# Rounding all rows of x and the second weights ahead of the squares of x, and splitting half of the v weights into another buffer

## The chip, the cores and the metric

The kernel runs on one core of a Trainium2 chip. The time is the device time of one execution in microseconds; several executions are made and their median is compared. The engines are named as in the profile: PE is TensorE's matmul, PEld its weight load, DVE is VectorE, ACT is ScalarE, POOL is GpSimd, SP is SyncE, which issues almost all DMA transfers here.

## The reference

One inference step of a hybrid decoder layer on 512 prompt tokens and 64 sample tokens, 576 in all, with 1024 features. What matters here is the beginning: the input is normalized and then projected by one wide weight matrix, of which the first pieces used are those of a gated linear recurrence (HGRN).

```python
def rms_norm(x, g):
    xf = x.astype(jnp.float32)
    y = xf * lax.rsqrt(jnp.mean(xf * xf, axis=-1, keepdims=True) + EPS)
    return (y * g.astype(jnp.float32)).astype(x.dtype)
...
def mixer_features(h, pos, lb, w_in, q_norm_g, k_norm_g):
    B, T, _ = h.shape
    z = h @ w_in
    offs = np.cumsum(IN_WIDTHS)[:-1].tolist()
    q_a, kv_c, kv_s, kv_w, gate_a, q_b, f_b, i_b, g_b, mg = jnp.split(z, offs, axis=-1)
...
    logf = jnp.log(lb + (1.0 - lb) * jax.nn.sigmoid(fz)).reshape(B, T, B_HEADS, B_KEY_DIM)
...
    qb = jax.nn.silu(q_b.astype(jnp.float32)).reshape(B, T, B_HEADS, B_KEY_DIM)
    vb = i_b.astype(jnp.float32).reshape(B, T, B_HEADS, B_VAL_DIM)
    gb = jax.nn.silu(g_b)
```

After it come the recurrence for four heads, sparse attention for prompt and samples, a merge and a gated feed-forward part with a short convolution.

## The kernel before

Activations are kept transposed: features on the 128 partitions in eight tiles (`KT`), tokens along the free dimension. The products need nearly float32 precision and use a two-part form: a value is rounded by ACT to the matmul's 32-bit format (the high part) and DVE or POOL subtracts to get the remainder (the low part). `split` (lines 326 to 334) issues both steps. A product is then three matmuls, high by high, high by low and low by high, listed by `THREE`, and `gemm` (line 360) makes 48 matmuls of 288 columns for one weight tile of 1024 x 128 against all 576 tokens.

`prep_x` (line 478) loads the eight rows of x, scales and rounds them (ACT line 333, DVE line 334), squares each one (ACT line 500) and adds the squares into two accumulators, those of even rows on DVE and those of odd rows on POOL (line 505). The token sums (line 451) and `token_rms` (line 454: mean squares on DVE, a power on POOL, line 463) give one factor per token. These factors do not enter the rounded x: the projections use unnormalized x and are multiplied by the factors afterwards. `spread` (line 466) carries the factors from partitions to columns: DVE writes a diagonal matrix `dg` (line 472), PE multiplies it with ones (lines 474 and 475), and DVE copies the result to `rsb`.

`hgrn` (line 806) then runs head by head: `hgrn_inputs` projects f with the weights wF and q with wQ, `hgrn_values` projects v for two heads with wI (lines 528 and 532), and a projection with wG gives the output gate. Weights come through `wload` into a ring of two raw buffers (`wraw`), and `wsplit` (line 341) splits them into a ring of two split buffers (`wsp`); every third split gives its remainder to POOL instead of DVE. For the first head wQ and wG do not use the ring: they are split into `phi` and `plo`, the two buffers that later hold the split pages of the compressed cache. wF of the first head is loaded and split inside `prep_x`; `wcols` (line 352) loads and splits wI in two halves of four feature tiles each.

The order on each engine is not the order of the source: the tile framework's scheduler arranges the instructions by its own estimates, and each engine then runs its list strictly in that order. `issue_after(i)` makes what is issued inside it follow instruction i in the scheduler's order. The list of SP is one queue: a transfer that must wait for a buffer holds those behind it.

Of the kernel before, what the change touches and what calls it, by code (L numbers as in the profile page):

```python
# [13 lines left out]
AF = mybir.ActivationFunctionType  # L14
# [8 lines left out]
KT = 8  # L23
# [201 lines left out]
QPL = "phi"  # L225
# [62 lines left out]
class Layer:  # L288
# [60 lines left out]
        self.split(sp[:, 0], sp[:, 1], raw, eng=nc.gpsimd if self.nsplit % self.pool_every == 0 else nc.vector)  # L349
        return sp  # L350

    def wcols(self, dram, cols):

        out = []
        for k in range(0, KT, 4):
            sp = self.wsplit(dram[:, k:k + 4], 4, cols)
            out += [sp[:, :, i] for i in range(4)]
        return out

# [118 lines left out]
    def prep_x(self, p):  # L478

        nc, a = self.nc, self.a  # L480
        self.xg = [Rows([self.xp.tile([128, 4, T], F32R, name="xg", tag=f"hi{i}") for i in range(2)]),
                   self.xp.tile([128, KT, T], F32R, name="xg", tag="lo")]
        self.xs = self.w1p.tile([128, KT, 2, 64], F32R, name="xs")
        self.rsb = self.xp.tile([128, T], F32, name="rsb", tag="rsb")
        self.rst = self.xp.tile([128, 5], F32, name="rst")
        acc = []
        for k in range(KT):
            x = p.tile([128, T], F32, name="x", tag="x", bufs=8)
            with self.tc.issue_after(self.wdma.ins) if k == 2 else nullcontext():
                nc.sync.dma_start(x, a["xT"][:, k])  # L490
            if k == 0:
                self.load_consts(self.cp, "base")
            if k == 1:
                self.w_first = self.wsplit(a["wF"][0], KT, 128)
            self.split(self.xg[0][:, k], self.xg[1][:, k], x, scale=self.small[:, k:k + 1])
            sq = p.tile([128, T], F32, name="sq", tag="z", bufs=6)
            if k in SQP:
                nc.gpsimd.tensor_tensor(sq, x, x, op=ALU.mult)
            else:
                nc.scalar.activation(sq, x, AF.Square)  # L500
            c = k % 2
            if k < 2:
                acc.append(sq)
            else:
                (nc.gpsimd if k in ADP else nc.vector).tensor_tensor(acc[c], acc[c], sq, op=ALU.add)
        ps = self.bank("ps")
        for i in range(2):
            self.token_sums(ps, acc[i], i == 0)
        for c in range(2):
            if c:  # L510
                nc.scalar.copy(self.xs[:, :, c, :], self.xg[c][:, :, TP:T].bitcast(F32))
            else:
                for i in range(2):
                    nc.scalar.copy(self.xs[:, 4 * i:4 * i + 4, c, :], self.xg[c].tiles[i][:, :, TP:T].bitcast(F32))
        rt = self.token_rms(p, ps, D)
        nc.vector.tensor_copy(self.rst, rt)
        pa, pb = self.spread(p, rt)
        nc.vector.tensor_copy(self.rsb[:, 0:512], pa)
        nc.vector.tensor_copy(self.rsb[:, 512:576], pb[:, 0:64])
        self.tap("rsb", self.rsb)  # L520
# [60 lines left out]
    def hgrn_inputs(self, p, h, q):  # L581

        nc, a = self.nc, self.a
        f = p.tile([128, T], F32, name="f", tag="f", bufs=2)
        k = p.tile([128, T], F32, name="k", tag="k", bufs=2)
        mv = p.tile([128, 144, 10], F32, name="mv", tag="mv")
        z = self.project(self.wsplit(a["wF"][h], KT, 128) if h else self.w_first, p, 1.0)
        th = p.tile([128, T], F32, name="th", tag="th", bufs=2)
        nc.scalar.activation(th, z, AF.Tanh, scale=0.5)
        nc.gpsimd.tensor_scalar(f, th, self.fb[:, h:h + 1], self.fa[:, h:h + 1], op0=ALU.mult, op1=ALU.add)  # L590
        nc.gpsimd.tensor_scalar(k, th, self.fbn[:, h:h + 1], self.fb[:, h:h + 1], op0=ALU.mult, op1=ALU.add)
        z = self.project(self.wsplit(a["wQ"][h], KT, 128, QPL and not h and (q, QPL)), p, 0.5, "g" if h else "lv")
        self.silu2(mv[:, :, 0:4], z, p, j=4)
        return f, k, mv

    def hgrn_values(self, p, x):

        w = self.wcols(self.a["wI"][x], 256)
        for j in range(5):
            ps = self.bank("ps")  # L600
            self.gemm_tok(ps, w, 256, j)
            d = self.vb[0:128 if j < 4 else 64, j, x].rearrange("p a b -> p (a b)")
            self.tok_out([(d, 0, 256)], ps, 256, j, p, "s1")
# [202 lines left out]
    def hgrn(self, p, q):  # L806
        nc, a = self.nc, self.a
        self.lm = p.tile([128, 1184], U8, name="lm")
        lmf = p.tile([128, 1184], F32, name="lmf", tag="mv")
        with self.tc.issue_after(self.wdma.ins):  # L810
            nc.sync.dma_start(lmf, a["lmask"])
        nc.vector.tensor_copy(self.lm, lmf)
        self.hgrn_consts()
        self.vb = p.tile([128, 5, 2, 2, 128], F32, name="vb")
        nxt = self.hgrn_inputs(p, 0, q)
        self.cmp = None
        for h in range(4):
            self.h = h
            if h % 2 == 0:
                self.hgrn_values(p, h // 2)  # L820
            gz = self.project(self.wsplit(a["wG"][h], KT, 128, GPL and not h and (q, GPL)), p, 0.5)
            if h == 0:
                with self.tc.issue_after(self.wdma.ins):
                    self.cmp_weights(q)
            gb = p.tile([128, T], F32, name="gb", tag="gb")
            self.silu2(gb, gz, p)
            if h == 0:
                self.cmp = self.cmp_sample(q)
            self.step(0)
            po = self.hgrn_chain(p, h, *nxt)  # L830
            if h == 0:
                self.cmp_pos(q)
            self.step(2)
            self.readout(p, h, *po, gb)
            if h < 3:
                nxt = self.hgrn_inputs(p, h + 1, q)
            self.gates_a(p, range(GA[h], GA[h + 1]))
            self.step(3)
            if h < 2:
                with self.tc.issue_after(self.page_dma.ins):  # L840
                    for b in range(4 * h, 4 * h + 4):
                        nc.sync.dma_start(self.o["wins"][b, 0:504, :], a["wst"][b, 8:512, :])

        for _ in self.cmp:
            pass
# [1058 lines left out]
```

## Time and profile before

| what | value |
|---|---|
| median of 3 executions | 1139.88 us (1139.77 to 1142.56) |
| profiled execution, its own time | 1141.99 us |
| its span, first to last instruction | 1140.2 us |
| PE busy | 1092.3 us, 96% of the span |
| DVE, ACT, POOL busy | 658.1, 470.8, 430.4 us |
| mean granted clock of PE | 0.985 |

The span is the stretch from the first to the last instruction of one profiled execution; the execution's own time has 1.8 us more, which lie around it. Times in the rows below are counted from the span's start. An engine that is busy for a small share can still hold PE up where its work stands in a chain ahead of PE's.

### The profile page before, as it was taken

What the parts mean: (1) busy time and instruction counts of PE and PEld (TensorE: products, weight loads), DVE (VectorE), ACT (ScalarE), POOL (GpSimd) and SP (SyncE); (2) the same over time, 40 slices, a digit from 0 to 9 for tenths busy, and PEclk for the clock granted to TensorE, in tenths of its full rate; (3) what the DMA queues carried; (4) which work ended last, traced back from release to release, by engine and by line L of the source; (5) the groups of instructions that cost most, each with busy time, mean ns of one, the idle gap of its engine ahead of it and who ended that gap; (6) DMA issues with size and microseconds to landing.
All of it is one profiled execution on the core that took longest, in us unless ns stands there. A gap on an engine that the chain in (4) does not pass through costs nothing.

```text
span 1140.2 us, 21336 instructions
## 1 busy us (share of the span) xinstructions
PE 1092.3 (96%) x7936; PEld 1034.8 (91%) x7936; DVE 658.1 (58%) x1182; ACT 470.8 (41%) x929; POOL 430.4 (38%) x514
## 2 busy tenths in 40 slices
PE   5999999999999899999888799999999999999998
PEld 5997999898999899899665699999999999999998
DVE  6768555674257756887776664665555555511110
ACT  5523443443444567776565643332223222311110
POOL 3654513833374535343365354232223222301010
PEclk8999899999999999999899999999999999999999
DMA  5634456454342422273789675322232223334330
GB/s 199 185 103 155 126 160 194 131 156 149 124 148 59 131 88 72 77 224 101 222 274 284 208 220 183 93 91 88 79 93 75 85 83 93 99 104 124 102 115 21
DMA packets 99273, 151.54 MB, mean 133 GB/s; under 512 B 11233, under 2 KB 66274, under 8 KB 99042
## 3 DMA queue, kind: packets, MB, share of 16 engines
q1 hardware_dynamic: 97714, 146.00, 41.2%
q0 software_dynamic: 1024, 3.54, 1.0%
q8 instruction: 62, 1.02, 0.4%
q10 hardware_dynamic: 432, 0.65, 0.2%
q14 instruction: 41, 0.34, 0.1%
HBM read 131.65 MB, written 22.62 MB: 135 GB/s over the span
## 4 chain that ended last, share of the span: by engine, by line
PE 60%; DVE 6%; ACT 2%; DMA 1%; issue 1%; POOL 1%; SPq 0%; DVEq 0%; ACTq 0%; POOLq 0%
PE ps_g L367 44%; PE ps_g L1200 2%; PE ps_hp L1307 2%; PE ps_sb L1299 2%; PE ps_po L1634 1%; DVE r L1138 1%; PE ps_sa L1267 1%; PE ps_g L1763 1%; PE ps_g L1773 1%; POOL rr L1128 1%; PE ps_sm L1333 1%; PE ps_g L1333 1%; DMA nraw<-in_wk 1%; PE ps_sa L1260 0%; PE ps_sc L1551 0%
## 5 line engine op out<-in xcount | busy, mean ns | idle before, releaser
L367 PE MATMUL ps_g<-h,wsp 128*128 128x288 f32 x2112 | 279.8, 294 | 0.0
L367 PEld LDWEIGHTS ps_g<-h,wsp 128*128 128x128 f32 x2112 | 279.4, 188 | 0.1
L330 ACT CAST wsp<-wraw 128x1024 fp32r<-128x1024 f32 (+3 forms) x142 | 136.3, 966 | 281.0 <-PE ps_g L367 240.5
L367 PE MATMUL ps_g<-xg,wsp 128*128 128x288 f32 x1200 | 182.9, 305 | 16.4 <-ACT wsp L330 8.8
L367 PEld LDWEIGHTS ps_g<-xg,wsp 128*128 128x128 f32 x1200 | 167.7, 193 | 23.6 <-ACT wsp L330 9.0
L331 DVE TENSOR_TENSOR wsp<-wraw,wsp 128x1024 fp32r<-128x1024 f32 (+2 forms) x93 | 113.5, 1222 | 116.4 <-ACT wsp L330 116.1
L331 POOL TENSOR_TENSOR wsp<-wraw,wsp 128x1024 fp32r<-128x1024 f32 (+3 forms) x49 | 108.0, 2203 | 187.1 <-ACT wsp L330 183.7
L367 PE MATMUL ps_g<-g,wsp 128*128 128x288 f32 x1056 | 140.9, 296 | 0.0
L367 PEld LDWEIGHTS ps_g<-g,wsp 128*128 128x128 f32 x1056 | 140.8, 189 | 0.0
L528 PE MATMUL ps_t<-wsp,xg 128*128 128x262 f32 (+1 forms) x480 | 60.9, 285 | 0.0
L528 PEld LDWEIGHTS ps_t<-wsp,xg 128*128 128x128 f32 x480 | 58.9, 189 | 0.1
L903 PE MATMUL ps_pc<-phi,w 128*128 128x256 f32 x256 | 51.0, 290 | 0.0
L330 ACT CAST phi<-praw 128x2048 fp32r<-128x2048 f32 x16 | 30.4, 1901 | 45.7 <-PE ps_pc L903 27.6
L1848 POOL COPY cout<-ext 128x2 f32<-128x2 f32 x22 | 4.1, 184 | 119.0 <-DVE ext L1845 119.0
L1155 POOL TENSOR_TENSOR zg<-zg,rsb 128x576 f32<-128x576 f32 x16 | 27.2, 1699 | 56.4 <-ACT zg L1154 56.4
L1863 DVE TENSOR_TENSOR s<-ps_g,s 128x576 f32<-128x576 f32 x22 | 16.6, 757 | 51.5 <-POOL s L1859 51.5
L1855 ACT ACTIVATE s<-cv 128x512 f32<-128x512 f32 x22 | 13.9, 632 | 78.6 <-DVE cv L1853 78.6
L331 DVE TENSOR_TENSOR plo<-praw,phi 128x2048 fp32r<-128x2048 f32 x14 | 32.7, 2338 | 22.4 <-ACT phi L330 22.2
L903 PEld LDWEIGHTS ps_pc<-phi,w 128*128 128x128 f32 x256 | 42.1, 196 | 0.8 <-issue 0.8
L1274 ACT ACTIVATE sP<-sP,nm 128x128 f32<-128x128 f32 (+3 forms) x64 | 35.6, 560 | 9.2 <-DVE nm L1272 9.2
L1844 DVE TENSOR_TENSOR ext<-ps_g,rs 128x288 f32<-128x288 f32 x22 | 10.1, 457 | 50.8 <-PE ps_g L367 50.7
L1859 POOL TENSOR_TENSOR s<-s,rs 128x576 f32<-128x576 f32 x22 | 31.6, 1434 | 18.8 <-ACT s L1858 18.8
(428 smaller groups left out, 1983.0 us busy)
## 6 DMA issues: line engine op xcount, KB each, us to landing
wraw<-in_wFi SPq DMA_DIRECT2D x44, 512.0 KB
praw<-in_pc SPq DMA_DIRECT2D x256, 64.0 KB
praw<-in_pkv SPq DMA_DIRECT2D x80, 128.0 KB
wraw<-in_wM SPq DMA_DIRECT2D x16, 512.0 KB
wraw<-in_wFo SPq DMA_DIRECT2D x16, 512.0 KB
gbd<-zg SPq DMA_DIRECT2D x24, 288.0 KB
wraw<-in_wBr SPq DMA_DIRECT2D x24, 256.0 KB
pgs<-in_pkv SPq DMA_DIRECT2D x48, 128.0 KB
```

The costliest lines, as they stand in the source:

```text
L330: self.copied = nc.scalar.copy(hi, src)
L331: (eng or nc.vector).tensor_tensor(lo, src, hi.bitcast(F32), op=ALU.subtract)
L367: self.last = nc.tensor.matmul(ps[:, h, 0:HF], w[:, cw, wk, :], (x[cx] if isinstance(x, list) else x[:, cx])[:, xk, h * HF:(h + 1) * HF], ...
L528: nc.tensor.matmul(ps[:, 0:n], self.xg[cx][:, k, j * 128:j * 128 + 128], w[k][:, cw], start=(k == 0 and c == 0), stop=(k == KT - 1 and c = ...
L903: self.nc.tensor.matmul(ps, self.w1[:, cw, j, k], x[cx][:, k], start=start and k == 0 and n == 0, stop=k == 7 and n == 2, skip_group_check ...
L1155: nc.gpsimd.tensor_tensor(z, z, self.rsb, op=ALU.mult)
L1200: self.last = nc.tensor.matmul(ps, w[:, cw, k], self.obs[cx][:, k, c], start=n == 0, stop=n == 11)
L1274: nc.scalar.activation(s[:, b], s[:, b], AF.Exp, scale=-1.0, bias=nm[:, 1 + b, i:i + 1], accum_out=sm[:, 1 + b, i:i + 1])
L1299: nc.tensor.transpose(ps[:, n * 128:n * 128 + 128], sP[i][:, b, j * 128:j * 128 + 128], self.cst("ident"))
L1307: last = nc.tensor.matmul(po[:, i * 128:512], vs[:, j, b].rearrange("p a d -> p (a d)"), pt[:, c, n * 128:(n + m) * 128], start=first, sto ...
L1333: self.last = nc.tensor.matmul(ps, w[:, cw, k], self.oas0[:, cx, k], start=n == 0, stop=n == 11)
L1859: nc.gpsimd.tensor_tensor(s, s, self.rs2, op=ALU.mult)
```

## The change

The squares of x leave the loop that rounds x. A second loop makes them, after all rows are rounded and after the second weights, wQ of the first head, are loaded and split; the squares on ACT are ordered behind the cast of wQ (`self.copied`). wQ of the first head now uses the ring's buffer instead of `phi`, and the second half of the first wI is split into `phi` instead of into the ring.

```diff
-    def wcols(self, dram, cols):
+    def wcols(self, dram, cols, place=None):
 
         out = []
         for k in range(0, KT, 4):
-            sp = self.wsplit(dram[:, k:k + 4], 4, cols)
+            sp = self.wsplit(dram[:, k:k + 4], 4, cols, place if k else None)
...
-        acc = []
+        acc, xs = [], []
         for k in range(KT):
...
             self.split(self.xg[0][:, k], self.xg[1][:, k], x, scale=self.small[:, k:k + 1])
+            xs.append(x)
+
+        self.w_second = self.wsplit(a["wQ"][0], KT, 128)
+        for k, x in enumerate(xs):
             sq = p.tile([128, T], F32, name="sq", tag="z", bufs=6)
             if k in SQP:
                 nc.gpsimd.tensor_tensor(sq, x, x, op=ALU.mult)
             else:
-                nc.scalar.activation(sq, x, AF.Square)
+                with self.tc.issue_after(self.copied.ins):
+                    nc.scalar.activation(sq, x, AF.Square)
...
-        z = self.project(self.wsplit(a["wQ"][h], KT, 128, QPL and not h and (q, QPL)), p, 0.5, "g" if h else "lv")
+        z = self.project(self.wsplit(a["wQ"][h], KT, 128) if h else self.w_second, p, 0.5, "g" if h else "lv")
...
-    def hgrn_values(self, p, x):
-
-        w = self.wcols(self.a["wI"][x], 256)
+    def hgrn_values(self, p, x, q):
+
+        w = self.wcols(self.a["wI"][x], 256, None if x else (q, QPL))
...
-                self.hgrn_values(p, h // 2)
+                self.hgrn_values(p, h // 2, q)
```

The scheduler makes another order of this. Three places follow; lines behind 494 are numbered five higher in the changed kernel.

PE at the beginning, before the change. `ps_g` is the f projection, `ps_lv` the q projection, lines 451 the token sums, 474 and 475 the spread, 528 wI:

```order
L367 MATMUL ps_g<-xg,wsp 128x288 x44
L451 MATMUL ps_ps<-c_base,sq 128x2 x4
L451 MATMUL ps_ps<-c_base,sq 64x2
L367 MATMUL ps_g<-xg,wsp 128x288 x4
L367 MATMUL ps_lv<-xg,wsp 128x288 x4
L451 MATMUL ps_ps<-c_base,sq 128x2 x4
L451 MATMUL ps_ps<-c_base,sq 64x2
L367 MATMUL ps_lv<-xg,wsp 128x288 x44
L474 MATMUL ps_ps<-dg,c_base 128x512
L475 MATMUL ps_ps<-dg,c_base 128x64
L528 MATMUL ps_ps<-wsp,xg 128x256 x96
```

and with the change:

```order
L367 MATMUL ps_g<-xg,wsp 128x288 x48
L367 MATMUL ps_lv<-xg,wsp 128x288 x48
L451 MATMUL ps_ps<-c_base,sq 128x2 x4
L451 MATMUL ps_ps<-c_base,sq 64x2
L451 MATMUL ps_ps<-c_base,sq 128x2 x4
L451 MATMUL ps_ps<-c_base,sq 64x2
L474 MATMUL ps_ps<-dg,c_base 128x512
L475 MATMUL ps_ps<-dg,c_base 128x64
L533 MATMUL ps_ps<-wsp,xg 128x256 x96
```

The token sums stood inside f and q, with 44 matmuls of q between them and the spread; now they stand behind both, directly ahead of the spread.

DVE around the factors, before the change, from the remainder of wQ (`wraw_277`) on. `wraw_341` is the second half of wI, `wraw_471` is wG, `rst` and `dg` are the factors and their diagonal matrix, `ptab` the page table:

```order
L331 TENSOR_TENSOR wsp_279<-wraw_277,wsp_279 128x1024
L461 TENSOR_SCALAR ms_173<-ps_ps_159 128x4
L462 TENSOR_SCALAR ms_173<-ps_ps_159 64x1
L516 COPY rst_97<-rt_174 128x5
L472 TENSOR_SCALAR dg_180<-c_base_100,rt_174 128x128 x4
L472 TENSOR_SCALAR dg_180<-c_base_100,rt_174 64x64
L331 TENSOR_TENSOR wsp_343<-wraw_341,wsp_343 128x1024
L857 TENSOR_SCALAR ptab_527<-praw_t_528 1x128
L331 TENSOR_TENSOR wsp_473<-wraw_471,wsp_473 128x1024
L518 COPY rsb_96<-ps_ps_186 128x512
```

and with the change, again from the remainder of wQ (now `wraw_137`) on:

```order
L331 TENSOR_TENSOR wsp_139<-wraw_137,wsp_139 128x1024
L510 TENSOR_TENSOR sq_142<-sq_142,sq_146 128x576
L510 TENSOR_TENSOR sq_142<-sq_142,sq_152 128x576
L510 TENSOR_TENSOR sq_142<-sq_142,sq_158 128x576
L331 TENSOR_TENSOR wsp_343<-wraw_341,wsp_343 128x1024
L461 TENSOR_SCALAR ms_178<-ps_ps_164 128x4
L462 TENSOR_SCALAR ms_178<-ps_ps_164 64x1
L862 TENSOR_SCALAR ptab_527<-praw_t_528 1x128
L331 TENSOR_TENSOR wsp_473<-wraw_471,wsp_473 128x1024
L521 COPY rst_97<-rt_179 128x5
L472 TENSOR_SCALAR dg_185<-c_base_100,rt_179 128x128 x4
L472 TENSOR_SCALAR dg_185<-c_base_100,rt_179 64x64
```

The remainders of wI's second half and of wG stood behind `dg`; now they stand ahead of it, that of wI also ahead of the mean squares `ms`.

POOL's additions of squares, before the change (`wraw_336` is the first half of wI):

```order
L505 TENSOR_TENSOR sq_115<-sq_115,sq_128 128x576
L505 TENSOR_TENSOR sq_115<-sq_115,sq_142 128x576
L505 TENSOR_TENSOR sq_115<-sq_115,sq_156 128x576
L331 TENSOR_TENSOR wsp_338<-wraw_336,wsp_338 128x1024
L463 TENSOR_TENSOR rt_174<-ms_173,mhalf_62 128x5
```

and with the change:

```order
L510 TENSOR_TENSOR sq_144<-sq_144,sq_149 128x576
L510 TENSOR_TENSOR sq_144<-sq_144,sq_155 128x576
L331 TENSOR_TENSOR wsp_338<-wraw_336,wsp_338 128x1024
L510 TENSOR_TENSOR sq_144<-sq_144,sq_161 128x576
L463 TENSOR_TENSOR rt_179<-ms_178,mhalf_62 128x5
```

The remainder of wI's first half moved ahead of the last addition.

## Rows read from the trace of the kernel before

**Rows 1.** The page, busy time of an engine, share of the span and instructions.
```profile
PE 1092.3 (96%) x7936; PEld 1034.8 (91%) x7936; DVE 658.1 (58%) x1182; ACT 470.8 (41%) x929; POOL 430.4 (38%) x514
```

**Rows 2.** Timeline of PE: start us, us, engine line op, out<-in, count, [idle before <-releaser].
```profile
7.88 6.37 PE L367 MATMUL ps_g<-xg,wsp 128*128 128x288 f32 x32 [7.88 <-ACT wsp L330]
15.76 1.85 PE L367 MATMUL ps_g<-xg,wsp 128*128 128x288 f32 x12 [1.51 <-DVE xg L334]
...
24.81 7.80 PE L367 MATMUL ps_lv<-xg,wsp 128*128 128x288 f32 x44
32.45 1.02 PE L474 MATMUL ps_ps<-dg,c_base 128*128 128x512 f32 x2
...
33.76 11.50 PE L528 MATMUL ps_ps<-wsp,xg 128*128 128x256 f32 x96
...
47.00 6.54 PE L367 MATMUL ps_g<-xg,wsp 128*128 128x288 f32 x48
53.38 1.24 PE L672 MATMUL ps_lv<-mv,k 128*128 128x320 f32 x4
```

**Rows 3.** Timeline of DVE, 8 to 44 us.
```profile
10.41 0.81 DVE L334 SCALAR_TENSOR_TENSOR xg<-x,small,xg 128x576 fp32r<-128x576 f32 x1
...
16.36 1.99 DVE L505 TENSOR_TENSOR sq<-sq 128x576 f32<-128x576 f32 x1
18.27 2.89 DVE L334 SCALAR_TENSOR_TENSOR xg<-x,small,xg 128x576 fp32r<-128x576 f32 x1
21.08 1.21 DVE L331 TENSOR_TENSOR wsp<-wraw,wsp 128x1024 fp32r<-128x1024 f32 x1
...
26.53 0.17 DVE L516 COPY rst<-rt 128x5 f32<-128x5 f32 x1 [1.32 <-POOL rt L463]
26.61 1.02 DVE L472 TENSOR_SCALAR dg<-c_base,rt 128x128 f32<-128x128 f32 x5
...
42.27 0.47 DVE L659 TENSOR_TENSOR mv<-mv,f 128x144 f32<-128x144 f32 x1
```

**Rows 4.** Timeline of POOL, 8 to 27 us.
```profile
10.81 1.70 POOL L505 TENSOR_TENSOR sq<-sq 128x576 f32<-128x576 f32 x1 [9.72 <-ACT sq L500]
...
17.97 2.57 POOL L331 TENSOR_TENSOR wsp<-wraw,wsp 128x1024 fp32r<-128x1024 f32 x1 [0.24 <-ACT wsp L330]
25.29 1.21 POOL L463 TENSOR_TENSOR rt<-ms,mhalf 128x5 f32<-128x5 f32 x1 [4.75 <-DVE ms L462]
```

**Rows 5.** Timeline of ACT, 8 to 30 us.
```profile
8.14 0.78 ACT L333 ACTIVATE xg<-x,small 128x576 fp32r<-128x576 f32 x1 [0.32 <-DMA x<-in_xT]
...
12.86 0.67 ACT L500 ACTIVATE sq<-x 128x576 f32<-128x576 f32 x1
13.43 0.76 ACT L333 ACTIVATE xg<-x,small 128x576 fp32r<-128x576 f32 x1
...
27.05 1.04 ACT L330 CAST wsp<-wraw 128x1024 fp32r<-128x1024 f32 x1 [5.23 <-DMA wraw<-in_wI]
28.47 1.05 ACT L330 CAST wsp<-wraw 128x1024 fp32r<-128x1024 f32 x1 [0.38 <-DMA wraw<-in_wG]
```

**Rows 6.** Timeline of SP's queue: the requests of wI's second half and of wG.
```profile
22.32 0.33 SPq L338 DMA_DIRECT2D wraw<-in_wI  x1
22.75 0.37 SPq L338 DMA_DIRECT2D wraw<-in_wG  x1
```

**Rows 7.** Stretches: length, busy us (count) by engine, PE's granted clock, DMA share, GB/s.
```profile
12.00:13.00 1.00, 1.00 (x10) 1.00 (x9) 1.00 (x1) 1.00 (x3) 0.51 (x1) 1.00 0.97 397
13.00:14.00 1.00, 1.00 (x9) 0.97 (x8) 1.00 (x3) 1.00 (x2) 0.33 (x1) 1.00 0.16 61
...
21.80:28.60 6.80, 6.80 (x32) 6.77 (x31) 2.29 (x10) 1.19 (x3) 1.21 (x1) 0.50 0.73 230
...
110.70:114.00 3.30, 0.91 (x8) 0.56 (x6) 3.25 (x5) 1.25 (x4) 3.13 (x2) 0.99 0.86 293
114.00:117.40 3.40, 3.40 (x15) 3.40 (x16) 3.13 (x7) 1.92 (x6) 3.26 (x5) 0.51 0.73 246
```

## The prediction

> **What bounds the kernel now.** I read the page's busy times first: the matmul engine PE is busy for 96% of the span [rows 1], so a change pays only where it takes away a wait of PE or a stretch at PE's lower clock. Then PE's row of the timeline for the first 67 us, the only place that the change works on [rows 2]. Up to 24.8 us PE is in pieces (after 32 matmuls of f it waits 1.51 us for x rounded by DVE, and later again). From 24.81 us it runs without a wait: 44 matmuls of the q projection, the spread of the row factors, then from 33.76 us 96 matmuls on the v weights (wI). Third, why x is late: DVE rounds a row in 0.81 us, but the last one takes 2.89 us and ends at 21.16, because POOL runs a two-input operation beside it; a sum of squares on DVE takes 1.99 us for the same reason [rows 3], and POOL's operations are stretched likewise [rows 4]. Each waits for the other's whole operation. Fourth, the clock: after this broken stretch the granted clock is 0.50 from 21.8 to 28.6 us [rows 7], so 6.8 us of PE run at 1.2 instead of 2.4 GHz.
>
> **What the change moves.** The same instructions are issued; only order and two buffers change. On ACT the eight squares go behind the casts of x and of wQ; on DVE the eight roundings then follow each other; on POOL the remainder of wI's first half goes ahead of the last addition; PE runs f and q without the token sums between them. I follow one chain through this order, with durations from rows.
>
> *x and q, earlier.* The third row of x is cast at 8.14 us, on its landing [rows 5]. At 397 GB/s [rows 7] a row of 0.29 MB takes 0.74 us, so the eighth is cast at 11.9, and DVE's roundings, 0.81 us each, end at about 13.7 instead of 21.16 us. wQ is the last transfer but one before the traffic stops between 13 and 14 us [rows 7], and 0.5 MB takes 1.3 us: it lands between 12 and 14; I take 13.1, as a late microsecond is covered below. Cast 1.04 us [rows 5], remainder on DVE 1.21 [rows 3]: usable at 15.4. PE did 32 matmuls of f by 14.25 us; the other 16 and the 48 of q cost 0.136 us each (6.54 us for 48 at 47.00 [rows 2]), so q ends at about 23.0 instead of 32.6 us. That lead of 9.6 us is worth nothing by itself: token sums and spread stand ahead of wI in PE's order.
>
> *Sums of squares, at the same time as before.* Squares start at 14.1 and come every 0.58 us (a square at 12.86 lets the next start at 13.43 [rows 5]); the fourth ends at 16.5, the sixth at 17.7. Then ACT casts xs (about 0.6, somewhat under a square of 0.67) and wI's first half, done at 19.2. POOL alone needs 1.70 - 0.41 = 1.29 us for an addition (DVE held it until 11.22) and 2.57 - 0.38 = 2.2 for a remainder (DVE held it until 18.35) [rows 3, 4]: two additions from 16.5 with one of DVE's between them to 19.7, remainder to 21.9, last addition to 23.8 after another turn of DVE. Token sums end near 24.8, mean squares at 25.2, POOL's power 1.21 us later [rows 4] at 26.5, as before.
>
> *The spread, held by another wait.* In the new DVE order the remainder of wG stands ahead of the copy of the factors and of dg. wG cannot be requested until POOL has finished wI's first half (one of two raw buffers): 22.0 us. Its landing is the main unknown. The transfer of wI's second half, at the head of an empty queue, took from 22.32 to 27.05 = 4.73 us; wG behind it from 22.75 to 28.47 = 5.72 us [rows 5, 6]. After the change wG is the one at the head (wI's second half leaves at 15.4), so I take 4.73: 26.7. Cast 1.05, remainder 1.21, factors and dg 1.10 (26.53 to 27.63 [rows 3]): dg ends at 30.1 and the spread starts at 30.2 instead of 32.45. **Gain 2.3 us**; with 5.72, and POOL's remainder 0.6 us later if DVE's addition goes first, 0.7.
>
> The order of those two turns is the place for a rule. Trainium skill, SBUF — State Buffer, "Who interferes with whom": a DVE instruction with two SBUF inputs and a GpSimd instruction that reads SBUF exclude each other, and the first to issue holds the port to its end. The stretched rows agree (2.89 us for 0.81 [rows 3]). By it POOL, free at 19.7 with its input there, goes ahead of DVE's third addition, whose square ends just behind; the other way the sum would be 0.6 us higher.
>
> *The clock, given back.* PE now idles from about 24.8 to 30.2 us. Before, a stretch of 3.3 us with 0.91 us of work was followed by 3.4 us at 0.51, and the broken beginning by 6.8 us at 0.50 [rows 7]. So the spread will run at half speed: its 1.31 us to the first wI matmul (32.45 to 33.76 [rows 2]) doubles, **cost 1.3 us** (bounds 0.6, if half of it is not matmul time, and 1.3). wI begins at 32.8 and stays slow until the clock returns: at once (0), or after as much as 6.8 us, which costs half of that, 3.4. I take 2.6 us of slow wI, **cost 1.3 us**, nearer to the stretch of 3.4 us, which also followed an idle PE.
>
> *Behind wI.* PE's rows from 33.76 to 60 us leave no idle time, so a shift of wI's end passes on. On DVE the next wF's remainder goes ahead of z, 1.2 us, and the level mask, whose transfer goes behind three page loads, may hold mv by as much again; the last piece of mv ended at 42.74 [rows 3] and PE reads it at 53.38 [rows 2], a cover of 10 us, so 0 (1 to 2 us if it were gone). The page loads start some 4 us sooner, but no PE row waits for one: 0. The phi buffer is free only when wI's products are done, so its first cast waits for them; its matmuls come behind 66 us: 0. Further on some rows of PE change places between 150 and 200 us. Neither gain nor loss is excluded; the nearest bound is the idle time of 110.7 to 114 us, 2.4 us [rows 7], either way; I take 0.
>
> **Sum:** -2.3 + 1.3 + 1.3 = +0.3 us. The profiled execution took 1141.99 us, so 1142.3; the median shown is 2.1 us lower, so I forecast 1140.2 us against 1139.88. A measurement of this kernel can tell about 0.3%, 3.4 us: this is no change.
>
> **Rivals.** *The lead is kept.* If wG lands earlier by 2.5 us or more, the spread waits only for POOL's power: it starts at 27.6 us, a gain of 4.8. With the spread's 1.3, and the clock back as wI starts (0), it is -3.5: **1136.4 us**. For it: wG has the queue to itself. Against it: the half-megabyte transfer at the head of an empty queue took 4.73 us. Trainium skill, DMA: Bandwidth & Descriptors, "Latency and other measured facts", gives 600 ns to the first byte for transfers that hardware queues issue; with the 435 GB/s of its specifications that is an estimate of 1.8 us for wG, which would make this rival true. The row of 4.73 us differs and decides.
>
> *The wait is longer than the lead* (the other side). wG takes 5.72 us and POOL's remainder goes second: a gain of 0.7 only. The spread's 1.3 and a wI that is slow for the full 6.8 us (3.4) give +4.0: **1143.9 us**. It decides from a spread later than about 31.7 with the clock at 0.50 past 38 us. For it: the clock stayed down that long after shorter waits. Against it: nothing is queued ahead of wG.
>
> *Nothing is moved that counts.* If wQ lands 2 us later than I take it, q ends at 25 and PE is still idle before the spread; if x is not sooner, likewise: 1140.2 again, within the forecast.
>
> **Chances.** Forecast with the third rival 0.63 (from its bounds its own range is -2.0 to +3.1 us); the lead kept 0.20; the longer wait 0.17. The 2.4 us behind 150 us can carry any of them over a bound, so the outer two are not smaller. The range takes the inside case, most of the first rival and half of the second: 1136.0 to 1143.8. Faster by over 0.3% 0.20, within it 0.63, slower 0.17.
>
> **What would show it.** In the new profile: DVE's eight roundings end near 14 us, none over 1 us; PE's f and q in one piece to about 23 us; wG's cast near 26.7 us, the idle time before it ended by its transfer; the spread near 30 us; a granted clock of 0.5 in 30 to 35 us; wI's 96 matmuls ending near 45.5 us, as before. Wrong would be: a spread before 28 us, or one that did not wait for wG; a full clock at 31 us; a PE wait of over 2 us behind 50 us that was not there.

## The result: 0.8% slower, and not at the beginning

The changed kernel takes 1151.18 us (median of 4 executions, 1148.67 to 1154.41), the kernel before 1139.83 us beside it (4 executions, 1138.75 to 1142.56): a ratio of 1.0076, 95% interval 1.0050 to 1.0102. That ratio stands for some 8.7 us; the two medians themselves lie 11.4 us apart. A second comparison (the run e11 below) gives 1.0076 again, 1.0051 to 1.0100. The forecast was 1140.2 us, range 1136.0 to 1143.8: the time lies outside, on the slow side.

The profiled execution of the changed kernel took 1148.71 us, its span is 1146.9 us, against 1141.99 and 1140.2. It is one of the two quicker executions of four; the other two took 1153.6 and 1154.4 us. First the page's busy times, which answer to [rows 1]:

```profile
PE 1093.9 (95%) x7936; PEld 1036.0 (90%) x7936; DVE 654.7 (57%) x1182; ACT 471.4 (41%) x929; POOL 427.3 (37%) x514
```

Of the 6.7 us that the span is longer, PE is busy 1.6 and idle 5.1. Where? Next the timeline of PE at the beginning, which answers to [rows 2] (columns as there; lines behind 494 have numbers five higher):

```profile
16.98 6.55 PE L367 MATMUL ps_lv<-xg,wsp 128*128 128x288 f32 x48
...
25.41 1.62 PE L451 MATMUL ps_ps<-c_base,sq 128*128 128x2 f32 x10 [0.89 <-POOL sq L510]
30.01 2.08 PE L474 MATMUL ps_ps<-dg,c_base 128*128 128x512 f32 x2 [2.98 <-DVE dg L472]
...
32.63 13.14 PE L533 MATMUL ps_ps<-wsp,xg 128*128 128x256 f32 x96
...
47.50 6.54 PE L367 MATMUL ps_g<-xg,wsp 128*128 128x288 f32 x48
```

f and q now run to 23.5 us with one wait of 0.27 us (at 9.95), the spread starts at 30.01 instead of 32.45, wI takes 13.14 instead of 11.50 us, and the f projection of the next head starts at 47.50 instead of 47.00. So the place that the change works on costs 0.5 us. The other 6.2 us of the profile come later. Two landmarks that both kernels have show where: the 16 matmuls of the third head's wI with `xs` (the columns of x of the sample tokens) start 0.65 us later than before, and the wG matmuls behind a wait of 0.85 us for z (a scaled projection), some 50 us on, start 6.9 us later. Before, from PE's timeline:

```profile
167.20 2.07 PE L532 MATMUL ps_ps<-wsp,xs 128*128 128x256 f32 x16
...
170.78 5.06 PE L367 MATMUL ps_g<-xg,wsp 128*128 128x288 f32 x36
...
192.90 1.16 PE L754 MATMUL ps_ps<-vb,kT 128*128 128x128 f32 x8 [0.87 <-ACT kT L746]
...
215.62 5.16 PE L367 MATMUL ps_g<-xg,wsp 128*128 128x288 f32 x37 [0.85 <-DVE z L557]
```

and after:

```profile
167.85 2.06 PE L537 MATMUL ps_ps<-wsp,xs 128*128 128x256 f32 x16
...
171.98 0.79 PE L367 MATMUL ps_g<-xg,wsp 128*128 128x288 f32 x4 [0.48 <-ACT wsp L330]
175.30 4.72 PE L367 MATMUL ps_g<-xg,wsp 128*128 128x288 f32 x22 [2.53 <-DVE wsp L331]
...
201.57 1.16 PE L759 MATMUL ps_ps<-vb,kT 128*128 128x128 f32 x8 [1.89 <-ACT kT L751]
...
222.54 4.76 PE L367 MATMUL ps_g<-xg,wsp 128*128 128x288 f32 x34 [0.85 <-DVE z L562]
```

The wG projection of the third head ran without a wait; now it waits 0.48 us for the weights' cast and 2.53 us for their remainder, and the state matmuls wait 1.89 us for kT (the transposed keys, which ACT copies) instead of 0.87. The view of stretches gives the whole of that piece (columns as in [rows 7]); before and after:

```profile
167.20:215.62 48.42, 45.72 (x333) 42.01 (x331) 26.38 (x41) 19.42 (x34) 24.72 (x24) 1.00 0.54 158
```

```profile
167.85:222.54 54.69, 48.94 (x332) 44.41 (x330) 25.86 (x41) 22.08 (x38) 28.92 (x30) 0.94 0.50 151
```

It is 6.3 us longer: PE idles 5.75 us instead of 2.70 (length less busy time), and is busy 3.2 us longer for the same work, because the granted clock is 0.94 instead of 1.00 (two stretches at half clock, one behind each wait):

```profile
176.20:179.70 3.50, 3.50 (x17) 3.50 (x16) 2.69 (x6) 0.00 (x0) 3.50 (x4) 0.51 0.51 129
...
207.00:210.40 3.40, 3.40 (x13) 2.45 (x12) 1.27 (x3) 1.61 (x4) 2.82 (x6) 0.50 0.61 202
```

Why is the remainder late? DVE's timeline before and after, from the last page remainder (`plo`) to the weights' remainder:

```profile
166.63 2.29 DVE L331 TENSOR_TENSOR plo<-praw,phi 128x2048 fp32r<-128x2048 f32 x1 [7.52 <-ACT phi L330]
...
169.85 1.23 DVE L331 TENSOR_TENSOR wsp<-wraw,wsp 128x1024 fp32r<-128x1024 f32 x1
171.11 0.42 DVE L544 TENSOR_TENSOR up<-ps_ps,up 64x256 f32<-64x256 f32 x1
171.45 0.41 DVE L676 TENSOR_TENSOR AT<-ps_lv,c_base 128x256 f32<-128x256 f32 x1
```

```profile
169.75 2.29 DVE L331 TENSOR_TENSOR plo<-praw,phi 128x2048 fp32r<-128x2048 f32 x1 [7.49 <-DMA praw<-in_pc]
...
172.96 0.42 DVE L681 TENSOR_TENSOR AT<-ps_lv,c_base 128x256 f32<-128x256 f32 x1
173.30 0.20 DVE L692 TENSOR_TENSOR ATs<-ps_ps,c_base 64x64 f32<-64x64 f32 x1
173.43 0.67 DVE L728 TENSOR_TENSOR Q<-Q,pt 128x512 f32<-128x512 f32 x1
174.03 1.21 DVE L331 TENSOR_TENSOR wsp<-wraw,wsp 128x1024 fp32r<-128x1024 f32 x1
```

The page remainder comes 3.1 us later, and three instructions (`AT` and `ATs`, two mask steps, and a product with `Q`) now stand ahead of the weights. Nothing in the source orders these; the scheduler's lists differ there. They differ between about 139 and 226 us of the kernel before and nowhere behind. On PE, 35 of wI's matmuls stand ahead of the 24 page matmuls instead of 14; on SP, wG's request stands ahead of a page's loads; on ACT, the copies of kT stand behind a page cast instead of ahead of it.

### The profile page after: what moved, and what is told of

The parts are those of the page before. It is cut to its first block, busy times and chain, and to the rows that moved or that the text cites. A ratio compares the mean times of both kernels' runs of the same rounds, so it can differ in the third digit from the quotient of the medians.

```text
span 1146.9 us, 21331 instructions
## 1 busy us (share of the span) xinstructions
PE 1093.9 (95%) x7936; PEld 1036.0 (90%) x7936; DVE 654.7 (57%) x1182; ACT 471.4 (41%) x929; POOL 427.3 (37%) x514
## 4 chain that ended last, share of the span: by engine, by line
PE 79%; DVE 7%; ACT 3%; DMA 3%; SPq 3%; issue 2%; POOL 2%; ACTq 0%; DVEq 0%; POOLq 0%
PE ps_g L367 51%; PE ps_t L533 3%; PE ps_pc L908 3%; SPq L935 2%; PE ps_g L1205 2%; PE ps_hp L1312 2%; PE ps_sb L1304 2%; PE ps_ps L533 2%; PE ps_g L1768 1%; PE ps_sa L1272 1%; PE ps_g L1778 1%; PE ps_lv L367 1%; DMA praw<-in_pkv 1%; DVE r L1143 1%; PE ps_po L1639 1%
## 5 line engine op out<-in xcount | busy, mean ns | idle before, releaser
L367 PE MATMUL ps_g<-xg,wsp 128*128 128x288 f32 x1200 | 187.4, 309 | 16.6 <-ACT wsp L330 9.8
L367 PEld LDWEIGHTS ps_g<-xg,wsp 128*128 128x128 f32 x1200 | 171.7, 197 | 23.8 <-ACT wsp L330 10.1
L331 DVE TENSOR_TENSOR wsp<-wraw,wsp 128x1024 fp32r<-128x1024 f32 (+2 forms) x93 | 117.4, 1263 | 117.8 <-ACT wsp L330 117.5
L1160 POOL TENSOR_TENSOR zg<-zg,rsb 128x576 f32<-128x576 f32 x16 | 26.5, 1657 | 59.9 <-ACT zg L1159 59.9
```

The lines of the kernel that those rows point to most:

```text
L331: (eng or nc.vector).tensor_tensor(lo, src, hi.bitcast(F32), op=ALU.subtract)
L367: self.last = nc.tensor.matmul(ps[:, h, 0:HF], w[:, cw, wk, :], (x[cx] if isinstance(x, list) else x[:, cx])[:, xk, h * HF:(h + 1) * HF], ...
L1160: nc.gpsimd.tensor_tensor(z, z, self.rsb, op=ALU.mult)
```

## The experiments

Theory A: the loss is this other order. Theory B: it is the beginning, by its clock. Theory C: it is the two buffers, since the pages use `phi`. To exchange only the order, a table gives each engine's instructions behind about 110 us in the order that the other kernel has, and an edge from each to the next binds the scheduler to it; the instructions keep their names in both kernels. Ratios are against the kernel before, run beside each, with 95% intervals; its medians there were 1141.35 us (e1 to e4), 1142.50 (e5 to e8), 1142.22 (e9 to e11) and 1141.68 (e12, e13).

**e1 and e2: the two halves of the program exchanged.**

```diff
+    def pin(self):
+
+        by = {i.name: i for i in self.nc.cur_bb.bb.instructions}
+        for order in PIN.values():
...
+            for x, y in zip(names, names[1:]):
+                self.tc.add_manual_dep(by[y], x, mybir.DependencyInfo(mybir.DependencyClass.NoSync, mybir.DependencyReason.DATA), reason="pin")
```

> The changed kernel, with the order of every engine behind about 110 us fixed to the order that the kernel before has there; the beginning, squares, buffers and all, stays changed. Theory A (the loss is in the rearranged order of the second pair of heads, 150 to 212 us): the median is within 1.5 us of before, 1139.5 to 1141.5, the 0.5 us by which PE ran late at 47 us is all that is left; no PE wait over 1 us between 150 and 200 us. Theory B (the beginning itself costs it, by the clock or by a later start of everything): the median stays at 1148 to 1152. Theory C (the two buffers that changed places cost it, since the pages use phi): it stays at 1148 to 1152 as well.

Measured: 1142.89 us, ratio 0.9997 (0.9976 to 1.0018). In the stretch of the landmarks PE idles 1.81 us, at full clock:

```profile
170.49:217.90 47.41, 45.60 (x332) 42.01 (x330) 26.35 (x41) 19.42 (x34) 24.69 (x24) 1.00 0.55 162
```

> The kernel before, with the order of every engine behind about 110 us fixed to the order of the changed kernel; its beginning and its buffers are untouched. Theory A: 8 to 11 us slower than before, 1148 to 1151, with a PE wait of some 2.5 us for the remainder of wG near 175 us. Theory B and theory C: within 1 us of before, 1139 to 1141.

Measured: 1148.21 us, ratio 1.0059 (1.0040 to 1.0078), and PE's waits between 168 and 216 us are nearly those of the changed kernel above (2.53, 1.89 and 0.48 us), from the view of the waits (what waited, for what, us in total, times, longest):

```profile
PE ps_g L388 <- DVE wsp L352: 2.5, 1, 2.5
PE ps_ps L776 <- ACT kT L768: 1.0, 1, 1.0
PE ps_g L388 <- ACT wsp L351: 0.5, 1, 0.5
```

The loss goes with the order behind 110 us and not with the beginning. Theory B falls.

**e3 and e4: the two edits of the change, each alone.** e3 exchanges only the buffers:

```diff
-            sp = self.wsplit(dram[:, k:k + 4], 4, cols)
+            sp = self.wsplit(dram[:, k:k + 4], 4, cols, place if k else None)
...
-        z = self.project(self.wsplit(a["wQ"][h], KT, 128, QPL and not h and (q, QPL)), p, 0.5, "g" if h else "lv")
+        z = self.project(self.wsplit(a["wQ"][h], KT, 128, None), p, 0.5, "g" if h else "lv")
...
-        w = self.wcols(self.a["wI"][x], 256)
+        w = self.wcols(self.a["wI"][x], 256, None if x else (q, QPL))
```

> The kernel before with nothing but the two buffers exchanged: wQ of the first head into the ring, the second half of the first wI into phi. PE's order comes out as before, from first to last. Theory A: within 1 us of before, 1139 to 1141. Theory B: the same. Theory C: most of the loss, 1146 to 1151, by a first page cast that waits for phi.

Measured: 1138.15 us, ratio 0.9962 (0.9948 to 0.9976). Theory C falls, and no theory had foreseen the gain of 4 us. DVE, POOL and the clock at the beginning show where it comes from (the last line is the view of stretches, as in [rows 7]):

```profile
19.25 0.81 DVE L334 SCALAR_TENSOR_TENSOR xg<-x,small,xg 128x576 fp32r<-128x576 f32 x1
...
22.52 2.43 POOL L331 TENSOR_TENSOR wsp<-wraw,wsp 128x1024 fp32r<-128x1024 f32 x1 [3.81 <-ACT wsp L330]
...
21.80:28.60 6.80, 6.80 (x54) 6.77 (x53) 2.46 (x9) 1.70 (x2) 3.61 (x2) 1.00 0.59 181
```

With wQ in the ring, the first half of wI must wait for the ring buffer of wF, so POOL's remainder runs at 22.52 instead of 17.97 us and no longer beside DVE's last rounding, which takes 0.81 us instead of 2.89 [rows 3, 4]. The spread starts at 28.77 instead of 32.45 us, and the f projection behind wI at 43.33 instead of 47.00. Of these 3.7 us the earlier rounding is the smaller part: the stretch that ran at half clock before runs at full clock here (54 matmuls instead of 32 from 21.8 to 28.6 us). From the last four matmuls of f to the spread PE takes 8.2 us instead of 11.2, which is 3.0 of the 3.7. That the clock held because PE's wait ahead of these matmuls is gone was not tried.

e4 keeps the new order and puts the buffers back:

```diff
-        self.w_second = self.wsplit(a["wQ"][0], KT, 128)
+        self.w_second = self.wsplit(a["wQ"][0], KT, 128, (q, QPL))
...
-        w = self.wcols(self.a["wI"][x], 256, None if x else (q, QPL))
+        w = self.wcols(self.a["wI"][x], 256)
```

> The change with its buffers undone: squares behind the casts of x and wQ as in the change, but wQ in phi and the second half of wI in the ring as before. PE's order comes out as that of the changed kernel, in the beginning and in the second pair. Theory A: 1148 to 1152, as the changed kernel. Theory B: the same. Theory C: within 1.5 us of before.

Measured: 1153.07 us, ratio 1.0089 (1.0060 to 1.0117). So the late squares alone bring the loss; the buffers alone bring a gain, which the change as a whole doesn't show. Nor does e1, with its old order behind 110 us: its f projection behind wI starts at 47.33, so with the late squares the gain of the buffers is gone at the beginning already.

**e5 and e6: one cause of the late remainder at a time.** e5 moves one instruction of DVE; e6 puts PE's list from 150 to 170 us back and the page cast ahead of a copy of v. In rows of their lists:

```diff
 L331 TENSOR_TENSOR plo<-praw,phi
+L331 TENSOR_TENSOR wsp<-wraw,wsp
...
 L728 TENSOR_TENSOR Q<-Q,pt
-L331 TENSOR_TENSOR wsp<-wraw,wsp
```

> The changed kernel, its order kept on every engine but for one instruction of DVE: the remainder of the third head's wG goes directly behind the page remainder, ahead of two additions of the page sums, two mask copies and a product with Q (2.07 us of DVE in the changed kernel, 171.96 to 174.03). If the page chain's 3.1 us of delay and these five operations add up (theory A, piece by piece), PE's wait of 2.53 us near 175 us shrinks to about 0.4 us, the low clock behind it may go with it, and the time is 2 to 4 us below the changed kernel: ratio to before 1.003 to 1.006. If the wait is set by something else (the cast on ACT, the landing of wG), it stays over 2 us and the ratio at 1.007 to 1.008.

Measured: 1147.47 us, ratio 1.0046 (1.0030 to 1.0062). The wait for the remainder is gone from PE's list of waits over 0.8 us, but 1.11 us for a page sum (at 177.7 us) and 2.25 us for kT (at 199.9 us) stand there now, and the stretch is as long as in the changed kernel (54.4 us). The ratio is nearer to 1 than the changed kernel's, though the intervals overlap.

> The changed kernel, its order kept but for PE between 150 and 170 us and one swap on ACT: as in the kernel before, 14 matmuls of wI instead of 35 stand ahead of the 24 page matmuls, and the page cast stands ahead of the first copy of v. Theory A: the next page loads, their cast and their remainder come 2.5 to 3.1 us sooner, so the wait for wG's remainder (2.53 us) is gone or under 0.5 us; what is left of the loss is the other rearrangement behind 175 us; ratio to before 1.001 to 1.005. If the delay came from SP's order (wG's request ahead of the page loads), the pages stay late, the wait stays over 2 us and the ratio at 1.006 to 1.009.

Measured: 1150.31 us, ratio 1.0068 (1.0053 to 1.0083). A miss: the page remainder came back to its old place, and the wait grew to 3.40 us:

```profile
170.60 2.29 DVE L352 TENSOR_TENSOR plo<-praw,phi 128x2048 fp32r<-128x2048 f32 x1 [7.52 <-DMA praw<-in_pc]
...
174.35 0.42 DVE L703 TENSOR_TENSOR AT<-ps_lv,c_base 128x256 f32<-128x256 f32 x1 [0.57 <-PE ps_lv L699]
...
174.99 2.76 DVE L750 TENSOR_TENSOR Q<-Q,pt 128x512 f32<-128x512 f32 x1
177.68 1.21 DVE L352 TENSOR_TENSOR wsp<-wraw,wsp 128x1024 fp32r<-128x1024 f32 x1
```

(This run is 3.97 us behind the kernel before at 169 us, so 170.60 answers to 166.63.) Now DVE waits for PE's own matmuls ahead of `AT`, and `Q` takes 2.76 us. The place of the remainder behind `AT`, `ATs` and `Q` is enough for the wait; the late pages are not needed.

**e9 and e10: one half of the order at a time,** by the same table (e9: the old order to about 175 us, e10: the old order behind it).

> The changed kernel, with the order of 140 to about 175 us (the page matmuls among those of wI, the remainder of the third head's wG among DVE's work, wG's request) as in the kernel before, and that of 175 to 212 us (the copies of kT behind the page cast on ACT, the page matmuls ahead of the key sums on PE) as in the changed kernel. If the loss is in the first group: ratio to before 0.998 to 1.002, no PE wait for the remainder of wG. If it is in the second: 1.004 to 1.008, with a PE wait of 1 to 2.5 us for kT near 200 us. If each costs its own part: 1.002 to 1.005.

Measured: 1150.37 us, ratio 1.0075 (1.0045 to 1.0105). The wait for the remainder is gone, that for kT is 2.49 us. ACT shows why, and then PE:

```profile
196.50 0.36 ACT L763 COPY AT<-ps_ps 64x256 f32<-64x256 f32 x1 [2.83 <-DVE AT L668]
196.84 1.90 ACT L351 CAST phi<-praw 128x2048 fp32r<-128x2048 f32 x1
...
199.53 0.58 ACT L773 COPY kT<-ps_ps 128x512 f32<-128x512 f32 x1
...
195.58 2.10 PE L388 MATMUL ps_g<-xg,wsp 128*128 128x288 f32 x14
200.17 1.16 PE L781 MATMUL ps_ps<-vb,kT 128*128 128x128 f32 x8 [2.49 <-ACT kT L773]
```

kT's input was there at 195.8 us, ACT waited for DVE and then cast a page first, and PE had 2.10 us of other work to cover it.

> The mirror of it: the order of 140 to 175 us as in the changed kernel, that of 175 to 212 us as in the kernel before. If the loss is in the first group: ratio to before 1.004 to 1.008, with PE's wait of 2 to 3.5 us for the remainder of wG. If it is in the second: 0.998 to 1.002, with that wait or without, since a later wait that is in both kernels then takes it up. If each costs its own part: 1.002 to 1.005.

Measured: 1148.65 us, ratio 1.0056 (1.0034 to 1.0078), with the wait of 2.53 us and none for kT. Each of the two results fits the branch that blames the half left in the new order, and the two branches exclude each other: each half of the order alone costs most of the loss or all of it, both together no more than one. The losses don't add.

**e11: the changed kernel again.**

> The changed kernel itself, unedited, beside the same runs of before, for a comparison on one chip: 1.005 to 1.010 of before.

Measured: 1151.86 us (1145.43 to 1155.31), ratio 1.0076 (1.0051 to 1.0100).

**e12 and e13: are two places the whole of it?** On ACT the copies of kT move up, in e12 with the first half old, in e13 with e5's move and nothing else:

```diff
+L751 COPY kT<-ps_ps
+L755 COPY kS<-ps_ps
 L741 COPY AT<-ps_ps
 L330 CAST phi<-praw
 L984 COPY cup<-ps_pc
 L985 COPY cup<-ps_pc
-L751 COPY kT<-ps_ps
-L755 COPY kS<-ps_ps
```

> The run with the first group in its old order, and one more move: on ACT the copies of kT and kS go ahead of the copy of AT, the page cast and two copies behind it, where the changed kernel has them behind these. In that run the matmuls that make kT's input ended at 195.8 us, ACT began the copy at 199.53 and PE waited 2.49 us. If this place on ACT is what the second group costs: the wait at 200 us is under 0.5 us, the stretch from 169 to 215 us loses under 2 us against before (6.2 in that run), ratio to before 1.000 to 1.004. If the second group costs something else (the order of its matmuls, the clock): the wait moves on to another operand, and the ratio stays at 1.005 to 1.009.

Measured: 1147.52 us, ratio 1.0041 (1.0016 to 1.0067). PE's waits in the stretch:

```profile
PE ps_pc L1029 <- DVE cpre L1016: 1.8, 1, 1.8
PE ps_pc L1023 <- DVE cpre L1016: 0.7, 1, 0.7
```

> The changed kernel with two moves and nothing else: the remainder of the third head's wG directly behind the page remainder on DVE, and the copies of kT and kS ahead of AT's copy and the page cast on ACT. If these two places carry the loss together: both waits (2.53 and 1.0 to 2.5 us) gone or under 0.6 us, ratio to before 1.000 to 1.004. If the late page loads cost as well: a wait of 1 us or more for the page sums (cpre) near 178 us stays, ratio 1.003 to 1.006.

Measured: 1150.10 us, ratio 1.0061 (1.0037 to 1.0086). The waits have gone to the page sums again:

```profile
PE ps_pc L1029 <- DVE cpre L1016: 2.3, 1, 2.3
PE ps_pc L1023 <- DVE cpre L1016: 1.1, 1, 1.1
...
```

Both waits can be taken away by one move each, and another operand is late in their place. The stretch between the landmarks (start of the `xs` matmuls to the wG matmuls behind the wait for z), each from the view of stretches, sums it up; idle is length less PE's busy time:

| run | length, us | PE idle, us | clock |
|---|---|---|---|
| before | 48.42 | 2.70 | 1.00 |
| e1, old order | 47.41 | 1.81 | 1.00 |
| changed | 54.69 | 5.75 | 0.94 |
| e11, changed again | 52.34 | 4.89 | 0.97 |
| e2, new order alone | 52.33 | 4.89 | 0.97 |
| e4 | 53.60 | 4.89 | 0.94 |
| e5, remainder moved | 54.44 | 5.15 | 0.94 |
| e6, pages moved | 54.15 | 5.28 | 0.94 |
| e9, first half old | 54.59 | 4.07 | 0.91 |
| e10, second half old | 51.28 | 4.27 | 0.97 |
| e12 | 52.36 | 3.41 | 0.93 |
| e13 | 55.09 | 5.16 | 0.91 |

Every list with a part of the new order makes the stretch 2.9 to 6.7 us longer, 0.7 to 3.1 us of it idle and the rest clock, for the same 330 matmuls; the whole old list doesn't (47.4 to 49.7 us in e1, e3, e7 and e8). That the order from 139 to 226 us makes the loss is shown (e1, e2). That one row of it does is refuted for the rows tried. Open is which set of rows would have to go back together, short of all. Open too is where the rest of the median loss lies: the stretch holds 6.3 us in the profile of the result and 3.9 in those of e2 and e11, of some 8.7.

**e7 and e8: the beginning without the other order.** With only the last three (e7) or four (e8) squares behind wQ's cast, the scheduler's order behind 110 us comes out as before:

```diff
-                with self.tc.issue_after(self.copied.ins):
+                with self.tc.issue_after(self.copied.ins) if k > 4 else nullcontext():
```

> The change with only the last three squares ordered behind wQ's cast; the first five go between the casts of x as they were. The token sums come out in the middle of q, the remainder of wG behind the diagonal matrix instead of ahead of it, and the order behind 110 us as in the kernel before. If the beginning could be made shorter without the rest being rearranged: the spread starts at 23 to 25 us instead of 30.0 (changed) or 32.45 (before), no PE wait over 1 us ahead of it, and the time is 1132 to 1136 (ratio 0.993 to 0.997). If a lead at the beginning is worth nothing (it is lost to the clock or to a later wait): 1138 to 1142.

Measured: 1138.20 us, ratio 0.9962 (0.9947 to 0.9977). The spread came later than expected, but no PE wait is left ahead of it:

```profile
23.02 4.59 PE L367 MATMUL ps_lv<-xg,wsp 128*128 128x288 f32 x22
27.44 1.02 PE L474 MATMUL ps_ps<-dg,c_base 128*128 128x512 f32 x2
```

> As the run with five early squares, but four: both token sums come together, after 26 matmuls of q, and the additions on DVE stand behind the remainder of wQ. Behind 110 us the order is that of the kernel before. If the lead counts: spread at 24 to 26 us, 1133 to 1137 (ratio 0.994 to 0.998). If it is lost later: 1138 to 1142.

Measured: 1139.13 us, ratio 0.9968 (0.9951 to 0.9985). So a form of the change that leaves the rest of the order alone is 0.3 to 0.4% faster than before. Both runs hold the exchanged buffers too, and these alone gain as much (e3, 0.9962). In the profiles the f projection behind wI starts at 42.01 us (e7) and 42.21 (e8) against 43.33 (e3), so the early rounding may add some 1.2 us; the times do not tell e7 and e8 from e3. With all squares late it gains nothing (e1).

## Why the prediction was wrong

Right were the beginning's steps. The eight roundings end at 14.3 us (forecast 13.7), q at 23.5 (23.0), the spread starts at 30.0 (30.2). The spread at half clock took 1.3 us longer, as forecast; wI took 1.6 us longer (1.3), as it was slow to 36.3 us, 3.7 us and not 2.6. The f projection behind wI starts 0.5 us later than before, where the sum said 0.3. The clock and wG's cast answer to [rows 7] and [rows 5]:

```profile
26.05:36.30 10.25, 7.27 (x27) 5.55 (x27) 8.36 (x18) 6.26 (x11) 2.32 (x10) 0.50 0.89 299
...
26.62 1.04 ACT L330 CAST wsp<-wraw 128x1024 fp32r<-128x1024 f32 x1 [5.22 <-DMA wraw<-in_wG]
```

The cast of wG, and with it the spread's start, fits by luck, as two errors cancel: wG was requested 1 us later than forecast (23.05) and took 3.57 us to its cast, not 4.73. And the spread had a second late operand, where the forecast saw one: DVE and POOL show it.

```profile
19.92 0.81 DVE L510 TENSOR_TENSOR sq<-sq 128x576 f32<-128x576 f32 x1 [1.10 <-ACT sq L505]
21.43 2.67 DVE L331 TENSOR_TENSOR wsp<-wraw,wsp 128x1024 fp32r<-128x1024 f32 x1 [0.70 <-ACT wsp L330]
...
27.69 1.23 DVE L331 TENSOR_TENSOR wsp<-wraw,wsp 128x1024 fp32r<-128x1024 f32 x1 [0.20 <-ACT wsp L330]
...
20.07 2.95 POOL L331 TENSOR_TENSOR wsp<-wraw,wsp 128x1024 fp32r<-128x1024 f32 x1
22.98 2.38 POOL L510 TENSOR_TENSOR sq<-sq 128x576 f32<-128x576 f32 x1
27.44 1.21 POOL L463 TENSOR_TENSOR rt<-ms,mhalf 128x5 f32<-128x5 f32 x1 [2.08 <-DVE ms L462]
```

DVE's third addition went ahead of POOL's remainder, by 0.15 us, and POOL's last addition took 2.38 us beside DVE's other remainder; so the power ended at 28.65 instead of 26.5 us, 0.3 us ahead of wG's remainder (28.92). Trainium skill, SBUF — State Buffer, "Who interferes with whom", lets the first to issue hold the port; the rows agree with that, and the forecast's error was who is first. So without wG in DVE's way the spread could have started at most 0.3 us sooner.

The first rival (the lead kept, 1136.4 us) and the second (a longer wait, with a spread past 31.7 us and half clock past 38) didn't happen: the half clock ended at 36.3 us. The range of -2.0 to +3.1 us that "Chances" gives to the forecast does not follow from its bounds, which make -1.7 to +2.4; nothing hangs on that.

**The step that failed** is the last of "Behind wI": "Further on some rows of PE change places between 150 and 200 us. ... I take 0", with a bound of 2.4 us from an idle stretch elsewhere [rows 7]. The place was seen, and costed by nothing that stands there. What the runs show in its place is 6.3 us in that stretch of the profile (3.9 in e11 and e2), half of it waits and half of it clock. The same step fails where the first paragraph calls the first 67 us "the only place that the change works on": e2, with the old beginning, is 0.6% slower. The bound was too small for two reasons. It was read on PE alone, while the rows that counted had moved on DVE (the remainder behind three others) and ACT (kT behind a page cast). And it held no clock: a wait of 2.5 us and the half clock behind it cost nearly twice the wait. What would have made the prediction wrong was named in its last sentence, a PE wait of over 2 us behind 50 us that was not there; it is the row at 175.30.

## What to carry to other kernels

Where a scheduler lays out the order, an edit's cost is not where the edit is: compare the lists of every engine to the end of the program, and for each place where they differ ask, on the engines that feed PE, which weight remainder or copy now stands behind something slower, and how much PE work covers it. To find out whether the rest of the program is to blame, bind its order to the other kernel's and exchange the two parts, the edited beginning and the rest; that settles in two runs what moving single instructions doesn't. If the idea is good at its own place, look for a form of it that leaves the rest of the order alone: here five early squares instead of none turned 0.8% slower into 0.4% faster. And try each part of an edit alone: here the two buffers by themselves gain as much.

## What the runs showed of the hardware

The clock can be half of such a loss or more. In e9 the stretch has 1.4 us more of idle time than before, and is 6.2 us longer, at a mean clock of 0.91. But a wait is neither needed nor enough: e7 and e8 idle under 1 us in it and show 0.96, and e3 waits 2.1 us for kT there at a clock of 1.00.

The same program's clock is not the same in each execution. Near 86 to 93 us, where no order differs, e1, e2 and e11 ran 6.8 us at half clock and lost 3.1 us; the profiles of before and of the changed kernel did not, and e11 is the changed kernel.

The profile of e11 (span 1152.9) lost some 4.5 us more between 560 and 660 us than that of the changed kernel above, where the wait for DVE in this row was 1.15 us:

```profile
587.16 0.50 PE L1639 MATMUL ps_po<-vc,pt 128*128 128x256 f32 x2 [3.36 <-DVE pt L331]
```

e10 had it too (2.73 us at 582.5). In the other profiles it is 0.9 to 1.5 us, in all five with the whole old order (before, e1, e3, e7, e8) and in eight of ten with new order. Two cases don't show whether the new order makes it likelier.
